# Mixing y as it is loaded, and sharing the mixing of x among three engines: a batched product x·yᵀ on one core

## The chip, the core and the metric

The kernel runs on one core of a Trainium2 chip. The metric is the device time in microseconds of one execution. The kernel before takes 303.1 us (three runs, 302.90 to 303.12). The span of a profile, counted from the first to the last recorded instruction, is slightly shorter (300.9 us for the kernel before).

## The reference

```python
batch, n_heads, seq_t, seq_s, channels = 8, 12, 512, 512, 64
# x, y: (8, 12, 512, 64) float32
def reference(x, y):
    return np.einsum('bhtc,bhsc->bhts', x, y).astype(np.float32)
```

There are 96 products of 512 x 64 by 64 x 512. The inputs have 25.2 MB, the output has 100.7 MB. The arithmetic is small: what counts is moving 125.8 MB. In the kernel before TensorE is busy with matmuls for 46% of the span, and the DMA queue fills 98.5% of it.

## The kernel before

Eight heads are one group; there are 12 groups, each made of two half groups (24 in all, numbered i), and each half group gives two results of 2 MB (48 in all). x and y of a group are loaded into one **slot**. There are five slots, and results are written into slots too, from which they are stored. The kernel's matmuls take the channels on the partitions, so x and y are rearranged ("mixed") within a partition by strided copies and then transposed on VectorE (2.06 us for one xT, 1.05 for one yT).

```python
    slots = ctx.enter_context(tc.tile_pool(name="slots", bufs=SLOTS))      # SLOTS = 5
    zeroed = [const.tile([P, K * E * D], u32, name=f"xb{half}") for half in range(2)]

    def load(g):
        both = slot()
        nc.sync.dma_start(both[:, :R * C], xv[g])
        nc.sync.dma_start(both[:, R * C:], yv[g])
        loaded[g] = both

    def compress(g):                       # frees the slot: ScalarE reads x, VectorE reads y
        both = loaded.pop(g)
        xk = kept.tile([P, R, C], bf16)
        yk = kept.tile([P, R, C], bf16)
        nc.scalar.activation(xk.rearrange("p r c -> p (r c)"), both[:, :R * C], COPY)
        nc.vector.tensor_copy(yk.rearrange("p r c -> p (r c)"), both[:, R * C:])
        inputs[g] = (xk, yk)

    def mix(i):                            # GpSimd alone: 4 copies of x, 2 of y
        # ... 4 x nc.gpsimd.tensor_copy(xb part <- xk part, 32 x 1024)
        # ... 2 x nc.gpsimd.tensor_copy(yb part <- yk part, 64 x 1024)

    def transposes(i):                     # VectorE: xT <- xb, yT <- yb
        # ...
        if i + 2 < 2 * NG:
            mix(i + 2)

    def result(o):                         # 8 matmuls, 4 evictions into a slot, then a store
        i, h = divmod(o, 2)
        otf = slot()
        # ... evictions of k = 0, 2, 6 on ScalarE, of k = 4 on VectorE
        if h == 0 and 2 <= i + 2 < 2 * NG:
            transposes(i + 2)
        return lambda: nc.sync.dma_start(ov[i, h], otf)

    with tc.manual_schedule():             # each engine's order is the order written here
        for g in range(SLOTS):
            load(g)
        # ... zeroing of xb
        stores = []
        for g in range(NG):
            compress(g)
            if g == 0:
                mix(0)
                mix(1)
            if g in (2, 4):
                transposes(g // 2 - 1)
            if g < 5:
                load(g + SLOTS)
            elif g in (5, 7, 9):
                stores.append(result(len(stores)))
            elif g in (6, 8):
                load(g // 2 + 7)           # groups 10 and 11
        for store in stores:
            store()
        for o in range(len(stores), 4 * NG):
            result(o)()
```

In the traces every engine runs its list in the order written (GpSimd in the kernel before: x copies from 7.51 us, y copies from 13.85, the next x copies from 17.47). And all loads and stores go through one queue (q1 of the page, 125.83 MB), in which the first stores stand behind the last load, that of group 11 (y issued at 50.41, the first store at 50.88).

Of the kernel before, what the change touches and what calls it, by code (L numbers as in the profile page):

```python
# [1 line left out]

# [4 lines left out]


@with_exitstack
def kernel(  # L10
    ctx: ExitStack,
    tc: tile.TileContext,
    x: bass.AP,
    y: bass.AP,
    out: bass.AP,
):









    nc = tc.nc
    B, H, T, C = x.shape
    _, _, S, _ = y.shape
    P = 128
    G = 8  # L30
    Q = P // G
    R = T // Q
    NG = B * H // G
    K = 8
    E = R // K
    D = 32
    SLOTS = 5
    fp32 = mybir.dt.float32
    bf16 = mybir.dt.bfloat16
    u32 = mybir.dt.uint32  # L40
    COPY = mybir.ActivationFunctionType.Copy
    assert C == 2 * D and S == T and R == D and Q * 2 == D

    xv = x.rearrange("b h t c -> (b h t c)").rearrange("(g p n) -> g p n", p=P, n=R * C)
    yv = y.rearrange("b h t c -> (b h t c)").rearrange("(g p n) -> g p n", p=P, n=R * C)
    ov = out.rearrange("b h t s -> (b h t s)").rearrange(
        "(o u h q n) -> o h q u n", u=2, h=2, q=Q * E, n=K * S
    )

    const = ctx.enter_context(tc.tile_pool(name="const", bufs=1))  # L50
    kept = ctx.enter_context(tc.tile_pool(name="kept", bufs=NG))
    slots = ctx.enter_context(tc.tile_pool(name="slots", bufs=SLOTS))
    ybpool = ctx.enter_context(tc.tile_pool(name="ybpool", bufs=2))
    tpool = ctx.enter_context(tc.tile_pool(name="tpool", bufs=3))
    pmpool = ctx.enter_context(tc.tile_pool(name="pmpsum", bufs=4, space=bass.MemoryType.PSUM))

    loaded, inputs, mixed, made = {}, {}, {}, {}
    zeroed = [const.tile([P, K * E * D], u32, name=f"xb{half}") for half in range(2)]

    def slot():  # L60
        return slots.tile([P, K * S], fp32, name="slot")
# [5 lines that stand above are left out]
        loaded[g] = both  # L67

    def compress(g):
        both = loaded.pop(g)  # L70
        xk = kept.tile([P, R, C], bf16)
        yk = kept.tile([P, R, C], bf16)
        nc.scalar.activation(xk.rearrange("p r c -> p (r c)"), both[:, :R * C], COPY)  # L73
        nc.vector.tensor_copy(yk.rearrange("p r c -> p (r c)"), both[:, R * C:])  # L74
        inputs[g] = (xk, yk)

    def mix(i):

        g, half = divmod(i, 2)
        xk, yk = inputs[g]  # L80
        xb = zeroed[half]
        xv2 = xb.bitcast(bf16).rearrange("p (k e c u) -> p k e c u", k=K, e=E, u=2)
        base = half * 64
        for ch in range(2):
            for u in range(2):
                lo = base + u * D
                nc.gpsimd.tensor_copy(  # L87
                    xv2[(2 * ch + u) * D:(2 * ch + u + 1) * D, :, :, :, u],
                    xk[lo:lo + D, :, ch * D:(ch + 1) * D].rearrange("p (e k) c -> p k e c", k=K),
                )  # L90
        yb = ybpool.tile([P, R // 2 * D], u32)
        yv2 = yb.bitcast(bf16).rearrange("p (j c w) -> p j w c", j=R // 2, w=2)
        for ch in range(2):
            nc.gpsimd.tensor_copy(  # L94
                yv2[ch * 64:(ch + 1) * 64],
                yk[base:base + 64, :, ch * D:(ch + 1) * D].rearrange("p (j w) c -> p j w c", w=2),
            )
        mixed[i] = (xb, yb)

    def transposes(i):  # L100
        xb, yb = mixed.pop(i)
        xT = tpool.tile([P, K * D * E], u32)
        nc.vector.transpose(  # L103
            xT.rearrange("p (k r e) -> p k e r", k=K, e=E),
            xb.rearrange("p (k e c) -> p k e c", k=K, e=E),
        )
        yT = tpool.tile([P, D * R // 2], u32)
        nc.vector.transpose(  # L108
            yT.rearrange("p (r j) -> p j r", r=D), yb.rearrange("p (j c) -> p j c", c=D)
        )  # L110
        made[i] = (xT.bitcast(bf16).rearrange("p (k h m) -> p k h m", k=K, h=2), yT.bitcast(bf16))
        if i + 2 < 2 * NG:
            mix(i + 2)

    def result(o):

        i, h = divmod(o, 2)
        xT, yT = made[i]
        otf = slot()
        ot = otf.rearrange("p (r s) -> p r s", s=S)  # L120
        for k in range(0, K, 2):
            pm = pmpool.tile([P, 2, S], fp32)
            for two in range(2):
                nc.tensor.matmul(  # L124
                    pm[:, two, :], xT[:, k + two, h, :], yT[:, h * S:(h + 1) * S], start=True, stop=True
                )
            if k == 4:
                nc.vector.tensor_copy(ot[:, k:k + 2, :], pm)  # L128
            else:
                nc.scalar.activation(ot[:, k:k + 2, :], pm, COPY)  # L130
        if h == 0 and 2 <= i + 2 < 2 * NG:
            transposes(i + 2)
        return lambda: nc.sync.dma_start(ov[i, h], otf)

    with tc.manual_schedule():
        for g in range(SLOTS):
            load(g)
        nc.vector.memset(zeroed[0], 0.0)  # L138
        nc.gpsimd.memset(zeroed[1], 0.0)  # L139
# [5 lines that stand above are left out]
                mix(1)  # L145
            if g in (2, 4):
                transposes(g // 2 - 1)
            if g < 5:
                load(g + SLOTS)
            elif g in (5, 7, 9):  # L150
                stores.append(result(len(stores)))
            elif g in (6, 8):
                load(g // 2 + 7)
# [6 lines that stand above are left out]
# [1 line left out]
_INS = ['x', 'y']  # L161
_OUTS = [((8, 12, 512, 512), 'float32')]


# [23 lines left out]
```

## Time and profile before

| | kernel before |
|---|---|
| time | 303.1 us |
| span of the profile | 300.9 us |
| the DMA queue's share of 16 engines' span | 98.5% |
| GpSimd busy | 202.4 us (67%) |
| ScalarE busy | 160.7 us (53%) |
| VectorE busy | 148.0 us (49%) |

A page of the profile cuts the span into 40 slices. A digit is the busy share of a slice in tenths, and the row GB/s is what the DMA moved in it. A row of a group reads: line, engine, operation, output <- input, shapes, count, then busy microseconds and mean nanoseconds of one, then the idle time in front of it and what ended it. A row of the timeline begins with start and duration in us. The lines themselves are in the prediction.

### The profile page before, as it was taken

How to read it: one execution, taken by the hardware profiler on the slowest of the kernel's cores; microseconds unless marked ns; L12 is line 12 of the kernel's file. 1: busy time of each engine (PE TensorE's matmuls, PEld its weight loads, DVE VectorE, ACT ScalarE, POOL GpSimd, SP SyncE). 2: the span in 40 equal slices, each digit the busy share in tenths (PEclk: the TensorE clock that was granted, in tenths of full speed). 3: DMA queues.
4: the chain of work that ended last, by engine and by line, in shares of the span. 5: the costliest groups of instructions: out<-in, count | busy, mean ns of one | idle time of the engine just before them, and what ended most of it. 6: DMA issues, size and time to landing. Idle time of an engine off the chain costs nothing.

```text
span 300.9 us, 1567 instructions
## 1 busy us (share of the span) xinstructions
PE 137.7 (46%) x377; PEld 46.9 (16%) x384; DVE 148.0 (49%) x109; ACT 160.7 (53%) x157; POOL 202.4 (67%) x149
## 2 busy tenths in 40 slices
PE   0004124465465456664646664547555845654000
PEld 0001001122121112221212121212121212211000
DVE  1565963858375546653574356535753475313000
ACT  4252558697473747465655565655556564647000
POOL 1999999998997787779776977797779720000000
PEclk9999987579877885577895586797785598775555
DMA  7999999999999999999999999999999999999993
GB/s 293 424 426 424 421 419 423 424 441 423 441 425 423 438 425 431 436 425 440 425 429 439 420 431 433 427 442 423 429 437 423 433 433 423 430 429 425 431 429 150
DMA packets 10377, 125.93 MB, mean 418 GB/s; under 512 B 1152, under 2 KB 1152, under 8 KB 1152
## 3 DMA queue, kind: packets, MB, share of 16 engines
q1 hardware_dynamic: 10368, 125.83, 98.5%
q8 instruction: 3, 0.05, 0.1%
q14 instruction: 6, 0.05, 0.0%
HBM read 25.17 MB, written 100.66 MB: 418 GB/s over the span
## 4 chain that ended last, share of the span: by engine, by line
DMA 82%; ACT 7%; issue 3%; ACTq 0%; DVE 0%; SPq 0%
DMA out_dram<-slot 65%; DMA slot<-in_y_dram 17%; ACT slot L130 7%; DVE yk L74 0%; ACTq L183 0%; SPq L65 0%; SPq L66 0%; ACTq L130 0%
## 5 line engine op out<-in xcount | busy, mean ns | idle before, releaser
L124 PE MATMUL pm<-yT,xT 128*128 128x512 bf16 x377 | 137.7, 516 | 137.9 <-ACT slot L130 112.5
L130 ACT ACTIVATE slot<-pm 128x1024 f32<-128x1024 f32 x144 | 137.0, 1024 | 96.2 <-DMA out_dram<-slot 88.3
L87 POOL COPY xb<-xk 32x1024 bf16<-32x1024 bf16 x96 | 134.5, 1401 | 37.1 <-DVE xT L103 27.5
L128 DVE COPY slot<-pm 128x1024 f32<-128x1024 f32 x48 | 58.7, 1224 | 101.5 <-DMA out_dram<-slot 100.4
L124 PEld LDWEIGHTS <-xT 128*128 128x128 bf16 x384 | 46.9, 122 | 227.7 <-issue 193.0
L94 POOL COPY yb<-yk 64x1024 bf16<-64x1024 bf16 x48 | 66.8, 1391 | 2.9
L103 DVE STREAM_TRANSPOSE xT<-xb 128x1024 uint32<-128x1024 uint32 x24 | 49.5, 2063 | 0.0
L73 ACT ACTIVATE xk<-slot 128x2048 bf16<-128x2048 f32 x12 | 23.0, 1913 | 21.1 <-DMA slot<-in_x_dram 21.1
L74 DVE CAST yk<-slot 128x2048 bf16<-128x2048 f32 x12 | 20.6, 1715 | 26.6 <-DMA slot<-in_y_dram 26.6
L108 DVE STREAM_TRANSPOSE yT<-yb 128x512 uint32<-128x512 uint32 x24 | 25.3, 1052 | 0.0
L73 ACT ACT_TABLE_LOAD x1 | 1.3, 1283 | 0.7 <-PEq L172 0.7
L138 DVE MEMSET xb<- 128x1024 uint32 x1 | 0.9, 912 | 1.0 <-PEq L172 1.0
L139 POOL MEMSET xb<- 128x1024 uint32 x1 | 1.0, 952 | 0.3 <-POOLq L172 0.3
L172 POOL MEMSET const-float32-0.0<- 128x1 f32 x1 | 0.1, 98 | 0.2 <-issue 0.2
L172 POOL MEMSET const-float32-1.0<- 128x1 f32 x1 | 0.1, 98 | 0.0
L172 POOL MEMSET const-bfloat16-1.0<- 128x1 bf16 x1 | 0.1, 98 | 0.0
L172 POOL MEMSET const-uint8-127<- 128x1 uint8 x1 | 0.1, 98 | 0.0
## 6 DMA issues: line engine op xcount, KB each, us to landing
out_dram<-slot SPq DMA_DIRECT2D x48, 2048.0 KB, 21.7
slot<-in_x_dram SPq DMA_DIRECT2D x12, 1024.0 KB, 18.1
slot<-in_y_dram SPq DMA_DIRECT2D x12, 1024.0 KB, 19.2
```

The source lines that it names most:

```text
L73: nc.scalar.activation(xk.rearrange("p r c -> p (r c)"), both[:, :R * C], COPY)
L74: nc.vector.tensor_copy(yk.rearrange("p r c -> p (r c)"), both[:, R * C:])
L87: nc.gpsimd.tensor_copy(xv2[(2 * ch + u) * D:(2 * ch + u + 1) * D, :, :, :, u], xk[lo:lo + D, :, ch * D:(ch + 1) * D].rearrange("p (e k) c ...
L94: nc.gpsimd.tensor_copy(yv2[ch * 64:(ch + 1) * 64], yk[base:base + 64, :, ch * D:(ch + 1) * D].rearrange("p (j w) c -> p j w c", w=2),)
L103: nc.vector.transpose(xT.rearrange("p (k r e) -> p k e r", k=K, e=E), xb.rearrange("p (k e c) -> p k e c", k=K, e=E),)
L108: nc.vector.transpose(yT.rearrange("p (r j) -> p j r", r=D), yb.rearrange("p (j c) -> p j c", c=D))
L124: nc.tensor.matmul(pm[:, two, :], xT[:, k + two, h, :], yT[:, h * S:(h + 1) * S], start=True, stop=True)
L128: nc.vector.tensor_copy(ot[:, k:k + 2, :], pm)
L130: nc.scalar.activation(ot[:, k:k + 2, :], pm, COPY)
L138: nc.vector.memset(zeroed[0], 0.0)
L139: nc.gpsimd.memset(zeroed[1], 0.0)
L172: nc = _bacc.Bacc("TRN2", target_bir_lowering=False, num_devices=1)
```

## The change

The intent is to relieve GpSimd, the busiest engine, which did all the mixing. The halves of y are now mixed straight out of the fp32 slot while loading: per group VectorE makes two copies, GpSimd one and ScalarE one. x of the first five half groups is still mixed by GpSimd. From the sixth on, VectorE makes two of the four copies, GpSimd one and ScalarE one. The mixing of x also moves within the order: from the transposes to the load stage and to behind each second result. `copy` in the cut below is a helper that calls `activation` on ScalarE and `tensor_copy` on the other engines; " ..." marks what is left out.

```diff
+    in_front = [nc.vector, nc.gpsimd, nc.vector, nc.scalar]
+    behind = [nc.vector, nc.gpsimd, nc.scalar, nc.vector]
 ...
     def compress(g):
         both = loaded.pop(g)
         xk = kept.tile([P, R, C], bf16)
-        yk = kept.tile([P, R, C], bf16)
         nc.scalar.activation(xk..., both[:, :R * C], COPY)
-        nc.vector.tensor_copy(yk..., both[:, R * C:])
+        ys = both[:, R * C:].rearrange("p (r c) -> p r c", c=C)
+        for half in range(2):
+            yb = kept.tile([P, R // 2 * D], u32, name=f"yb{half}")
+            for ch in range(2):
+                copy(in_front[2 * half + ch], yb part, ys part)
 ...
     def mix(i):
         for ch in range(2):
             for u in range(2):
-                nc.gpsimd.tensor_copy(xb part, xk part)
+                copy(nc.gpsimd if i < 5 else behind[2 * ch + u], xb part, xk part)
-        # two nc.gpsimd.tensor_copy of y
 ...
     def transposes(i):
-        if i + 2 < 2 * NG:
-            mix(i + 2)
 ...
     def result(o):
-        if h == 0 and 2 <= i + 2 < 2 * NG:
+        if h == 0 and i + 2 < 2 * NG:
             transposes(i + 2)
+        elif h == 1 and i + 4 < 2 * NG:
+            mix(i + 4)
 ...
             if g in (2, 4):
                 transposes(g // 2 - 1)
+                mix(g // 2 + 1)
```

More of the change, by code (lines that the diff above doesn't have):

```diff
@@ L52 @@
     slots = ctx.enter_context(tc.tile_pool(name="slots", bufs=SLOTS))
-    ybpool = ctx.enter_context(tc.tile_pool(name="ybpool", bufs=2))
     tpool = ctx.enter_context(tc.tile_pool(name="tpool", bufs=3))
@@ L58, with copy @@
     zeroed = [const.tile([P, K * E * D], u32, name=f"xb{half}") for half in range(2)]
+    in_front = [nc.vector, nc.gpsimd, nc.vector, nc.scalar]
+    behind = [nc.vector, nc.gpsimd, nc.scalar, nc.vector]
+    def copy(engine, dst, src):
+        if engine is nc.scalar:
+            nc.scalar.activation(dst, src, COPY)
+        else:
+            engine.tensor_copy(dst, src)
     def slot():
@@ L71, in compress @@
         xk = kept.tile([P, R, C], bf16)
-        yk = kept.tile([P, R, C], bf16)
         nc.scalar.activation(xk.rearrange("p r c -> p (r c)"), both[:, :R * C], COPY)
-        nc.vector.tensor_copy(yk.rearrange("p r c -> p (r c)"), both[:, R * C:])
-        inputs[g] = (xk, yk)
+        inputs[g] = xk
+        ys = both[:, R * C:].rearrange("p (r c) -> p r c", c=C)
+        for half in range(2):
+            yb = kept.tile([P, R // 2 * D], u32, name=f"yb{half}")
+            yv2 = yb.bitcast(bf16).rearrange("p (j c w) -> p j w c", j=R // 2, w=2)
+            for ch in range(2):
+                copy(
+                    in_front[2 * half + ch],
+                    yv2[ch * 64:(ch + 1) * 64],
+                    ys[half * 64:(half + 1) * 64, :, ch * D:(ch + 1) * D].rearrange(
+                        "p (j w) c -> p j w c", w=2
+                    ),
+                )
+            mixed[2 * g + half] = yb
     def mix(i):
         g, half = divmod(i, 2)
-        xk, yk = inputs[g]
-        xb = zeroed[half]
-        xv2 = xb.bitcast(bf16).rearrange("p (k e c u) -> p k e c u", k=K, e=E, u=2)
-        base = half * 64
+        xk = inputs[g]
+        xv2 = zeroed[half].bitcast(bf16).rearrange("p (k e c u) -> p k e c u", k=K, e=E, u=2)
         for ch in range(2):
             for u in range(2):
-                lo = base + u * D
-                nc.gpsimd.tensor_copy(
+                lo = half * 64 + u * D
+                copy(
+                    nc.gpsimd if i < 5 else behind[2 * ch + u],
                     xv2[(2 * ch + u) * D:(2 * ch + u + 1) * D, :, :, :, u],
@@ L90, in mix @@
                 )
-        yb = ybpool.tile([P, R // 2 * D], u32)
-        yv2 = yb.bitcast(bf16).rearrange("p (j c w) -> p j w c", j=R // 2, w=2)
-        for ch in range(2):
-            nc.gpsimd.tensor_copy(
-                yv2[ch * 64:(ch + 1) * 64],
-                yk[base:base + 64, :, ch * D:(ch + 1) * D].rearrange("p (j w) c -> p j w c", w=2),
-            )
-        mixed[i] = (xb, yb)
     def transposes(i):
-        xb, yb = mixed.pop(i)
+        xb, yb = zeroed[i % 2], mixed.pop(i)
         xT = tpool.tile([P, K * D * E], u32)
```

## The prediction

The sum came to 307.0 us: 303.1 for the kernel before, and 3.85 us of starvation. "Lock" is the word for the time that a copy of one engine adds to a copy of the other; the traces show that time and not the mechanism behind it. That the new VectorE copies (the "them" behind the second cut) add it as the CAST does was an assumption, and 0.4 us for each was estimated from the 0.9 of the CAST. Rival A is the case that they add nothing.

> **What bounds the kernel now.** I read the page first (slices, queues, chain of waits), then the groups by line, the waits of the DMA queue, and the timeline of the first 64 us, where the change acts most.
>
> From the page:
>
> ```profile
> DMA  7999999999999999999999999999999999999993
> GB/s 293 424 426 424 421 419 423 424 441 423 441 425 423 438 425 431 436 425 440 425 429 439 420 431 433 427 442 423 429 437 423 433 433 423 430 429 425 431 429 150
> ...
> q1 hardware_dynamic: 10368, 125.83, 98.5%
> ...
> DMA 82%; ACT 7%; issue 3%; ACTq 0%; DVE 0%; SPq 0%
> ...
> L87 POOL COPY xb<-xk 32x1024 bf16<-32x1024 bf16 x96 | 134.5, 1401 | 37.1 <-DVE xT L103 27.5
> ...
> L94 POOL COPY yb<-yk 64x1024 bf16<-64x1024 bf16 x48 | 66.8, 1391 | 2.9
> ...
> out_dram<-slot SPq DMA_DIRECT2D x48, 2048.0 KB, 21.7
> ```
>
> The DMA rows carry the verdict: between first and last slice no slice falls under 9 tenths, and the one busy queue fills 98.5% of 16 engines' span. 125.83 MB at the 420 to 442 GB/s of the middle slices is some 290 to 295 us of a 300.9 us span; the rest is start and tail. GpSimd, busiest of the engines (202.4 us, 67%), is not the bound. A store lands 21.7 us after its issue although 2 MB at 430 GB/s takes 4.9 us, so about four transfers are always queued: in the store stage an engine may be many microseconds late and the DMA notices nothing. Relieving GpSimd therefore buys nothing by itself. The change can only move the time by letting the DMA queue run empty, and that must be looked for in the load stage, where queue and slots are shared by loads and first results.
>
> The timeline, first its issues and landings, then single GpSimd and VectorE instructions:
>
> ```profile
> 0.74 0.39 SPq L65 DMA_DIRECT2D slot<-in_x_dram  x1
> 5.54 1.91 ACT L73 ACTIVATE xk<-slot 128x2048 bf16<-128x2048 f32 x1 [3.53 <-DMA slot<-in_x_dram]
> 8.00 1.90 DVE L74 CAST yk<-slot 128x2048 bf16<-128x2048 f32 x1 [6.07 <-DMA slot<-in_y_dram]
> ...
> 32.86 2.05 DVE L74 CAST yk<-slot 128x2048 bf16<-128x2048 f32 x1 [0.18 <-DMA slot<-in_y_dram]
> 35.07 2.85 ACT L130 ACTIVATE slot<-pm 128x1024 f32<-128x1024 f32 x3 [2.77 <-DVE yk L74]
> ...
> 40.28 0.33 SPq L65 DMA_DIRECT2D slot<-in_x_dram  x1
> ...
> 50.04 0.33 SPq L65 DMA_DIRECT2D slot<-in_x_dram  x1
> ...
> 60.21 1.91 ACT L73 ACTIVATE xk<-slot 128x2048 bf16<-128x2048 f32 x1 [1.41 <-DMA slot<-in_x_dram]
> ```
>
> ```profile
> 7.51 1.31 POOL L87 COPY xb<-xk 32x1024 bf16<-32x1024 bf16 x1 [5.83 <-ACT xk L73]
> 8.86 2.22 POOL L87 COPY xb<-xk 32x1024 bf16<-32x1024 bf16 x1
> ...
> 47.77 1.23 DVE L74 CAST yk<-slot 128x2048 bf16<-128x2048 f32 x1 [1.16 <-DMA slot<-in_y_dram]
> ```
>
> Read there: a load issued alone at 0.74 lands at 5.54, 4.8 us. One y lands every 4.97 us (8.00 for group 0, 32.86 for group 5). Group 5's slot is free at 34.9 and goes to result 0 at 35.07. The last two loads are issued at 40.28 (group 10) and 50.04 (group 11), and x of group 11 lands at 60.21 in an unbroken stream. So it must be issued by about 60.2 - 4.8 = 55.4; before, there are 5.4 us to spare. The stores are issued only behind these loads, in program order, so nothing else can fill a hole.
>
> [...] a GpSimd copy takes 1.31 us, but 2.22 where a CAST became ready at 8.00; the CAST takes 1.90 there, 1.23 at 47.77. Each CAST costs GpSimd 0.9 us. [...] I take them to lock as the CAST does; no run yet shows it. [...]
>
> **The change part by part.**
> Removed: 12 VectorE casts (20.6 us) and 48 GpSimd y copies (66.8 us). Added: 48 y copies out of the fp32 slot, 24 on VectorE, 12 on ScalarE, 12 on GpSimd. The 96 x copies stay, but GpSimd does 4 x 5 + 19 = 39, VectorE 38, ScalarE 19. Estimates for one: VectorE 0.6 us (half of 1.23), [...] GpSimd 1.35 (from start to start, 7.51 to 8.86). GpSimd falls to about 51 x 1.35 = 69 us, [...] VectorE gains 62 x 0.6 - 20.6 = 17 us. All stay well under the span. Per pair of results, 9.8 us of DMA, VectorE needs 2 x 1.22 + 2.06 + 1.05 + 2 x 0.6 = 6.8 [...]. So the store stage is still hidden: worth nothing either way.
>
> Moved: a slot is now free only when GpSimd too has copied its y part out of it. GpSimd works in order, and its list puts the x copies of the first five half groups between: y0, mix 0, mix 1, y1, y2, mix 2, y3, y4, mix 3, y5, y6, y7, mix 4, y8. Up to y5 that is 16 + 6 = 22 copies, 22 x 1.36 = 29.9 us from 8.0. To it come the locks of 12 VectorE copies: the CAST cost 0.9, one of half the length about 0.4, in sum 4.8. So y5 ends at about 8.0 + 29.9 + 4.8 = 42.7, and result 0, which needs this slot, starts there in place of 35.07.
>
> Behind it ScalarE and VectorE also work in order. ScalarE: result 0 42.8 to 45.7, x6 to 47.6, [...]. VectorE: eviction to 44.0, transposes (2.05 + 1.05) to 47.2, then four y copies of groups 6 and 7, alternating with the copies of mix 4 on GpSimd, which starts when the first transpose frees xb at 46.2: they end at about 48.1, 49.8, 51.6 and 53.3. Group 6's slot is free at 49.8, so load 10 is issued then: 49.8 + 4.8 = 54.6, while unbroken its x would land at 60.2 - 4.97 = 55.2. Just in time. Result 1 needs group 7's slot: ScalarE 53.4 to 56.25, x8 to 58.15, [...]. Only now is group 8's slot free for load 11: issued at 59.25, x landed at 64.05 against 60.2. **The DMA is starved for 3.85 us** around 57 to 61 us. After that results 0 and 1 are ready to go, and each further result needs 2.85 us of evictions against 4.9 of transfer, so the queue fills again and the loss is neither repeated nor won back.
>
> Sum: 303.1 + 3.9 = 307.0 us.
>
> **The rivals.**
> A: no loss. [...] y5 ends at 37.9, load 11 is issued 4.8 us earlier still through ScalarE's chain [...], inside 55.4, and the time is 303. For it: the destination has a step of 4 bytes, unlike the CAST. [...]
> B: a larger loss. If the two engines alternate worse (0.55 per lock) or GpSimd's fp32 source costs it more than 1.35, y5 ends at 44 to 45, load 10 is late by 1 as well and load 11 by 5: 308.5 to 310.
> C: a gain, since GpSimd is 67% busy and loses 130 us of work. Against it: the DMA rows; the most that is left is start and tail, which the change does not touch. 302 to 303.
> D: the store stage starves as VectorE gets the x copies. Against it: 6.8 of 9.8 us and four queued stores.
>
> **Range and chances.** The step in the middle has a width of about 2 us: without the wait for group 7's copies on VectorE the hole is 2 us, with worse alternation 5.5. Rival A gets 15 to 20%, so the range reaches down to it: 302.8 to 309.3. 2% slower is 309.2, the upper end of rival B: 0.13. 2% faster would be 297, which leaves the DMA a span of 295 us, its bare 290 to 295 without start and tail: 0.01. Within 2%: 0.86.
>
> **What would show it.** In the changed profile: result 0's first eviction at about 43 and not at 35; the loads of groups 10 and 11 issued at about 50 and 59; in the slices a dip of DMA and GB/s in the eighth or ninth (52 to 68 us), some 4 us deep, and none later; in the queue's waits ScalarE or GpSimd of the y copies as what the last load waited for; GpSimd copies at 1.7 us in the load stage, 1.31 later; VectorE y copies of 0.6 us alone and up to 1.9 contended; store latency again about 21.7. I am wrong if the DMA rows have no dip (rival A or C), if load 11 is issued before 55, or if a dip lies in the store stage (D).

## The result

The changed kernel takes 308.24 us (median of four runs, 307.99 to 308.51), beside 303.01 us for the kernel before on the same chip. The ratio is 1.0174, with a 95% interval from 1.0156 to 1.0192. Ratios in this document are the mean time of one kernel's fast runs over the mean of the other's of the same rounds, so they are not quite the ratio of the medians quoted. The loss of 1.7% is under 2%, but it is far outside the noise.

From the page of the changed kernel, the slices, the queue and the groups that answer to those shown of before:

```profile
DMA  7999999499999999999999999999999999999994
GB/s 288 427 422 424 421 421 409 200 325 430 425 439 421 434 434 421 443 419 436 435 419 443 421 432 434 424 443 417 437 425 432 434 424 430 428 426 439 417 436 205
...
q1 hardware_dynamic: 10368, 125.83, 97.3%
...
L66 POOL COPY xb<-xk 32x1024 bf16<-32x1024 bf16 x39 | 57.0, 1461 | 147.5 <-DVE xT L114 146.5
...
L66 DVE CAST yb<-slot 64x1024 bf16<-64x1024 f32 x24 | 33.2, 1384 | 12.6 <-DMA slot<-in_y_dram 12.3
...
L66 DVE COPY xb<-xk 32x1024 bf16<-32x1024 bf16 x38 | 27.8, 732 | 0.5
...
L66 POOL CAST yb<-slot 64x1024 bf16<-64x1024 f32 x12 | 17.7, 1511 | 17.7 <-DMA slot<-in_y_dram 17.5
L64 ACT ACTIVATE yb<-slot 64x1024 bf16<-64x1024 f32 x12 | 15.9, 1326 | 3.6 <-DMA slot<-in_y_dram 3.4
...
out_dram<-slot SPq DMA_DIRECT2D x48, 2048.0 KB, 21.6
```

The DMA row has one dip, in the eighth slice (a slice is 7.66 us, so 53.6 to 61.3 us); the GB/s stay low through the ninth. Before and behind it the rows read as in the kernel before, and a store still lands 21.6 us after its issue. GpSimd is indeed relieved, from 202.4 us busy to 75.9, and the time went up.

The timeline of the changed kernel, its results, loads and the copies between:

```profile
43.39 2.85 ACT L139 ACTIVATE slot<-pm 128x1024 f32<-128x1024 f32 x3 [9.09 <-POOL yb L66]
...
50.65 0.33 SPq L73 DMA_DIRECT2D slot<-in_x_dram  x1
...
54.16 2.85 ACT L139 ACTIVATE slot<-pm 128x1024 f32<-128x1024 f32 x3 [1.35 <-DVE yb L66]
...
58.97 1.33 ACT L64 ACTIVATE yb<-slot 64x1024 bf16<-64x1024 f32 x1
...
60.37 0.33 SPq L73 DMA_DIRECT2D slot<-in_x_dram  x1
```

Read these as a chain. ScalarE sits idle for 9.09 us before result 0, until GpSimd's y copy of group 5 has read the slot; the result starts at 43.39 where it started at 35.07 before. Result 1 follows at 54.16, held by VectorE's y copies of group 7. ScalarE's y copy of group 8 ends at 60.30, and only then is the load of group 11 issued, at 60.37 where it was 50.04.

The waits of the changed kernel's DMA queue (waited for: us in total, times, longest) name the same holders:

```profile
SPq L73 <- DVE yb L66: 24.2, 4, 13.6
...
SPq L73 <- POOL yb L66: 17.7, 4, 8.8
...
SPq L73 <- ACT yb L64: 2.5, 1, 2.5
```

Nine waits of the loads now end with some engine's y copy; the one load that waited for ScalarE is the last. Most of this waiting is harmless, since the DMA was busy all the same: the DMA row has a 9 in every slice but the first, the eighth and the last.

What it costs is seen by stretches. The columns are the stretch, its length, each engine's busy time and instructions, the granted TensorE clock, the DMA's busy share and its GB/s. The kernel before:

```profile
57.00:62.00 5.00, 1.79 (x5) 0.47 (x4) 2.29 (x3) 3.59 (x2) 4.86 (x4) 0.76 1.03 431
62.00:70.00 8.00, 5.62 (x17) 1.95 (x18) 6.69 (x6) 8.00 (x10) 6.71 (x5) 0.79 1.03 442
80.00:280.00 200.00, 113.52 (x309) 38.48 (x313) 100.28 (x76) 114.64 (x121) 132.10 (x101) 0.74 1.01 430
```

The changed kernel:

```profile
57.00:62.00 5.00, 1.55 (x5) 0.43 (x4) 3.29 (x4) 4.93 (x4) 1.79 (x1) 0.84 0.16 33
62.00:70.00 8.00, 3.57 (x8) 1.13 (x8) 6.25 (x6) 7.82 (x8) 0.83 (x1) 0.60 1.01 363
80.00:280.00 200.00, 112.41 (x330) 39.00 (x337) 133.35 (x118) 143.85 (x145) 23.81 (x18) 0.80 1.01 430
```

In the 5 us from 57 to 62 the DMA moves 33 GB/s in place of 431, which is 5 x 398 / 430 = 4.6 us of transfer lost. In the 8 us behind, it is busy but moves 363 in place of 442, another 8 x 79 / 430 = 1.5 us. Together that is 6.1 us; the span grew by 5.5 us, and the 0.6 us between them are not accounted for. In the 200 us of the store stage both move 430 GB/s, although VectorE and ScalarE carry 30 us more each there.

### The profile page after: what moved, and what is told of

Same layout as the page of the kernel before. It is cut to its first block, busy times and chain, and to the rows that moved or that the text cites. A ratio compares the mean times of both kernels' runs of the same rounds, so it can differ in the third digit from the quotient of the medians.

```text
span 306.4 us, 1486 instructions
## 1 busy us (share of the span) xinstructions
PE 132.8 (43%) x377; PEld 45.5 (15%) x384; DVE 188.9 (62%) x159; ACT 202.2 (66%) x188; POOL 75.9 (25%) x56
## 4 chain that ended last, share of the span: by engine, by line
DMA 56%; ACT 15%; issue 1%; ACTq 0%
DMA out_dram<-slot 56%; ACT slot L139 12%; ACT xk L81 1%; ACT yb L64 1%; ACT xb L64 1%; ACTq L195 0%; ACTq L139 0%
## 5 line engine op out<-in xcount | busy, mean ns | idle before, releaser
L133 PE MATMUL pm<-yT,xT 128*128 128x512 bf16 x377 | 132.8, 496 | 148.2 <-ACT slot L139 115.9
L66 POOL COPY xb<-xk 32x1024 bf16<-32x1024 bf16 x39 | 57.0, 1461 | 147.5 <-DVE xT L114 146.5
L133 PEld LDWEIGHTS <-xT 128*128 128x128 bf16 x384 | 45.5, 119 | 234.6 <-issue 196.9
L114 DVE STREAM_TRANSPOSE xT<-xb 128x1024 uint32<-128x1024 uint32 x24 | 49.8, 2076 | 0.7
L66 DVE CAST yb<-slot 64x1024 bf16<-64x1024 f32 x24 | 33.2, 1384 | 12.6 <-DMA slot<-in_y_dram 12.3
L66 DVE COPY xb<-xk 32x1024 bf16<-32x1024 bf16 x38 | 27.8, 732 | 0.5
L64 ACT ACTIVATE xb<-xk 32x1024 bf16<-32x1024 bf16 x19 | 25.4, 1335 | 0.5
L66 POOL CAST yb<-slot 64x1024 bf16<-64x1024 f32 x12 | 17.7, 1511 | 17.7 <-DMA slot<-in_y_dram 17.5
L64 ACT ACTIVATE yb<-slot 64x1024 bf16<-64x1024 f32 x12 | 15.9, 1326 | 3.6 <-DMA slot<-in_y_dram 3.4
## 6 DMA issues: line engine op xcount, KB each, us to landing
out_dram<-slot SPq DMA_DIRECT2D x48, 2048.0 KB, 21.6
```

Source lines behind the costliest of these rows:

```text
L64: nc.scalar.activation(dst, src, COPY)
L66: engine.tensor_copy(dst, src)
L114: nc.vector.transpose(xT.rearrange("p (k r e) -> p k e r", k=K, e=E), xb.rearrange("p (k e c) -> p k e c", k=K, e=E),)
L133: nc.tensor.matmul(pm[:, two, :], xT[:, k + two, h, :], yT[:, h * S:(h + 1) * S], start=True, stop=True)
```

## The experiments

**The theory:** the time is that of the DMA, and the change costs one hole in its queue, because the last load is issued too late. It is late because a slot now waits for GpSimd's in-order list, and behind it for ScalarE's and VectorE's. **Rival 1:** the store stage pays, as VectorE and ScalarE carry the x copies there. **Rival 2:** the engines' accesses slow the transfers themselves. A further question was how much of GpSimd's delay comes from its list and how much from copies that take longer beside VectorE's (2.22 us in place of 1.31 in the kernel before).

| run | what | time | before, same rounds | ratio [95%] | last load issued |
|---|---|---|---|---|---|
| – | the changed kernel | 308.24 | 303.01 | 1.0174 [1.0156, 1.0192] | 60.37 |
| e1 | store 0 ahead of the last load | 303.64 | 303.07 | 1.0027 [1.0006, 1.0048] | 60.30 |
| e2 | y part alone | 308.39 | 303.07 | 1.0183 [1.0166, 1.0200] | 60.42 |
| e3 | x part alone | 302.76 | 303.07 | 0.9990 [0.9975, 1.0005] | 50.09 |
| e4 | GpSimd mixes 3 half groups of x, not 5 | 306.10 | 303.07 | 1.0100 [1.0085, 1.0115] | 57.46 |
| e5 | no y copies on VectorE | 314.86 | 303.26 | 1.0385 [1.0369, 1.0400] | 64.74 |
| e6 | no y copies on GpSimd | 304.18 | 303.26 | 1.0040 [1.0024, 1.0055] | 55.98 |
| e7 | kernel before, store 0 ahead | 303.37 | 303.26 | 1.0007 [0.9990, 1.0023] | 50.40 |
| e8 | kernel before, slot of group 8 held longer | 307.79 | 303.26 | 1.0152 [1.0136, 1.0167] | 58.76 |
| e9 | e1 and e6 together | 303.03 | 302.88 | 0.9998 [0.9981, 1.0014] | 55.91 |

All gave correct results. e1 to e4 ran on one chip, e5 to e8 on another, e9 on a third; each is compared with the kernel before on its own chip.

### e1: one DMA issue moved

```diff
             elif g in (6, 8):
+                if g == 8:
+                    stores.pop(0)()
                 load(g // 2 + 7)
 ...
```

(Cut: the numbers of the results, which the kernel takes from the length of `stores`, are written out in two more lines.)

> The changed kernel with one DMA issue moved: the store of result 0 goes out ahead of the last load (group 11). All engine instructions stay as they are. My theory (one hole in the DMA queue, because the last load is issued at 60.4 while the loads before it end at 58.0): result 0 is evicted at 46.3 in the profile of the changed kernel, so its store (4.9 us of DMA) can be issued right behind load 10 at about 51.5 and bridges 58.0 to 62.9; the last load still goes out at about 60.4. The dip in the slices is gone and the time is 302.8 to 303.6, within 0.2% of before. Rival 1 (the store stage pays, as VectorE and ScalarE carry more there): nothing changes, 308. Rival 2 (the transfers themselves are slowed by more engine accesses): nothing changes, 308.

The time is 303.64 us, the engines' instructions being those of the changed kernel in the same order. The timeline of the queue:

```profile
51.41 0.64 SPq L144 DMA_DIRECT2D out_dram<-slot  x1
60.30 0.33 SPq L73 DMA_DIRECT2D slot<-in_x_dram  x1
```

The last load is as late as before the edit, and nearly all of the loss is gone. So the engines' work and their collisions cost time only through the hole: what counts is whether the DMA has something to do from 57 to 62 us. Rivals 1 and 2 fall. The time is just above the range that I had expected, and 0.6 us above the kernel before; e7 and e9 take that up. Also missed: the dip in the slices is not gone. The DMA is busy throughout, but the eighth slice moves 317 GB/s:

```profile
GB/s 295 432 419 428 422 416 419 317 416 436 426 432 429 434 429 434 425 436 427 426 436 432 434 421 432 432 429 425 435 420 432 434 419 434 429 425 427 423 438 217
```

### e2 and e3: one part of the change at a time

```diff
 # e2
-                    nc.gpsimd if i < 5 else behind[2 * ch + u],
+                    nc.gpsimd if i < 24 else behind[2 * ch + u],
```

> The y part of the change alone: y is mixed at load by three engines as in the changed kernel, but GpSimd does all 24 half groups of x, so VectorE and ScalarE do no x copies. My theory: until 60 us the instruction lists are those of the changed kernel, so the same hole: 308.0 to 308.6, last load issued at 60.4. Rival 1 (the store stage pays for the x copies on VectorE and ScalarE): these are gone, 303 to 305.

e3 takes y back to the way of the kernel before (one cast per group on VectorE while loading, the two strided copies on GpSimd later) and leaves the sharing of x as changed.

```diff
 # e3, in compress and mix (shortened)
-        # four copies of y out of the slot, on three engines
+        yk = kept.tile([P, R, C], bf16)
+        nc.vector.tensor_copy(yk..., both[:, R * C:])
 ...
+            nc.gpsimd.tensor_copy(yb part, yk part)     # twice per half group
```

> The x part alone: x copies shared as in the changed kernel, y as before (VectorE casts the whole group at load, GpSimd mixes it later out of the bf16 copy). My theory: a slot is free again as soon as ScalarE and VectorE have read it, result 0 starts at about 35, the last load goes out at about 50, no hole: 302.8 to 303.6. Rival 1 (store stage): 307 to 308.

e2 gives 308.39 us, the whole loss, though all x copies are back on GpSimd. e3 gives 302.76 us, with x shared through the whole store stage: the same as before within the noise. The loss is in the y part, and nothing of it is in the store stage.

### e4: a dose

```diff
-                    nc.gpsimd if i < 5 else behind[2 * ch + u],
+                    nc.gpsimd if i < 3 else behind[2 * ch + u],
```

> A dose: GpSimd alone mixes x of 3 half groups in place of 5; the others are shared 2:1:1. My theory: 3 copies fewer on GpSimd before y of group 5 (3 x 1.36 = 4.1 us, less the locks of two more VectorE copies): it ends at about 39.5 in place of 43.4. Behind it one more copy of 1.33 on ScalarE and fewer locks: last load at about 56.4 in place of 60.4, the hole is about 1 us in place of 5: 303.6 to 305. Rivals 1 and 2: more copies on VectorE and ScalarE, so 308 or more.

The direction is right, the size was missed: 306.10 us, where I expected 303.6 to 305. From the timeline of e4:

```profile
38.53 1.74 DVE L66 CAST yb<-slot 64x1024 bf16<-64x1024 f32 x1
...
40.56 1.23 DVE L137 COPY slot<-pm 128x1024 f32<-128x1024 f32 x1 [0.30 <-DVE yb L66]
```

GpSimd's list is shorter, but the two x copies that VectorE got stand ahead of its y copies of group 5. Each of these four runs beside GpSimd's copies and takes 1.6 to 1.75 us, so the slot comes free at 40.3 by VectorE, after GpSimd's copy, which ended at 39.7 (I had worked out 39.5). The last load went out at 57.46 where I had worked out 56.4. I had counted the delay for GpSimd and not for VectorE.

### e5: how much VectorE's copies slow GpSimd's

```diff
-    in_front = [nc.vector, nc.gpsimd, nc.vector, nc.scalar]
+    in_front = [nc.scalar, nc.gpsimd, nc.scalar, nc.scalar]
```

> The changed kernel with the two y copies of VectorE per group given to ScalarE, so that VectorE runs no SBUF copy in the load stage. [...] My theory: every GpSimd copy up to y of group 5 takes 1.31 (in the changed kernel about half took 1.7 to 1.8), so it ends at 8.2 + 22 x 1.36 = 38.1 in place of 43.4. The time gets worse all the same, since ScalarE now needs 1.91 + 3 x 1.33 = 5.9 us per group against 4.97 of loading: y of group 5 ends there at 41.6, and through its list (result 0, x6, y6, x7, y7, result 1, x8, y8) the last load is issued at 65.0, some 9.8 us after the 55.2 at which it would still be seamless: 312.5 to 314. Rival (GpSimd's order alone decides, no lock): GpSimd's copies keep their 1.7 to 1.8.

GpSimd's first two copies in the timeline of the changed kernel (the second row merges two):

```profile
8.22 1.78 POOL L66 CAST yb<-slot 64x1024 bf16<-64x1024 f32 x1 [6.54 <-DMA slot<-in_y_dram]
10.06 3.06 POOL L66 COPY xb<-xk 32x1024 bf16<-32x1024 bf16 x2
```

The same in e5, and the copies of y of groups 5 and 6 (merged in the last row):

```profile
8.14 1.30 POOL L66 CAST yb<-slot 64x1024 bf16<-64x1024 f32 x1 [6.46 <-DMA slot<-in_y_dram]
9.50 2.66 POOL L66 COPY xb<-xk 32x1024 bf16<-32x1024 bf16 x2
...
36.53 2.67 POOL L66 CAST yb<-slot 64x1024 bf16<-64x1024 f32 x2
```

Without a VectorE copy beside it, each GpSimd copy takes 1.31 us, and y of group 5 ends at about 37.9. In the changed kernel it ends at about 43.4. The difference of 5.5 us is what VectorE's copies cost GpSimd; the prediction estimated 4.8 for it. So of the 8.3 us by which result 0 starts later than in the kernel before (43.39 beside 35.07), about 5.5 come from the two engines slowing each other and only 2.8 from the length of GpSimd's list. The time, 314.86 us, is worse than the 312.5 to 314 expected. The last load went out at 64.74, as worked out (65.0). But in e5's page the twelfth slice is low as well:

```profile
GB/s 291 432 420 420 423 424 421 117 206 379 436 320 434 417 418 436 429 415 431 433 431 419 426 429 431 419 425 432 431 415 433 431 430 417 423 431 433 421 429 283
```

A second hole near 86 to 94 us (320 in place of about 430 in a slice of 7.8 us, so 2 us) is large enough for what I had missed. The timeline of e5 shows what came before it: ScalarE was still copying y until 85.1, evicted result 3 only from 85.12 on, and its store went out at 88.01, 14 us behind the store of result 2. My sum stopped at the last load.

### e6: GpSimd out of the slot's way

```diff
-    in_front = [nc.vector, nc.gpsimd, nc.vector, nc.scalar]
+    in_front = [nc.vector, nc.scalar, nc.vector, nc.scalar]
```

> The changed kernel with GpSimd's y copy given to ScalarE (VectorE and ScalarE two each), so that a slot no longer waits for GpSimd. If GpSimd's in-order list were the whole cause: result 0 starts at 36.7 and the time is 303. By my arithmetic ScalarE's list then becomes the limit: result 0 36.7 to 39.6, x6 41.5, two y6 44.2, x7 46.1, two y7 48.7, result 1 51.6, x8 53.5, two y8 56.1: last load at about 56.2, 1 us late, plus up to 1 us for loads and stores that start together: 304 to 305.

The time is 304.18 us, inside the range worked out. From the timeline of e6:

```profile
36.38 2.86 ACT L139 ACTIVATE slot<-pm 128x1024 f32<-128x1024 f32 x3 [0.74 <-DVE yb L66]
...
49.75 1.50 DVE L66 CAST yb<-slot 64x1024 bf16<-64x1024 f32 x2
...
53.29 2.67 ACT L64 ACTIVATE yb<-slot 64x1024 bf16<-64x1024 f32 x2
55.98 0.33 SPq L73 DMA_DIRECT2D slot<-in_x_dram  x1
```

Result 0 starts at 36.4, 7 us sooner, and still the last load is late by half a microsecond: ScalarE's own list is now what holds the slot of group 8. So waiting for GpSimd's copy is the larger cause, but not the only one. In each of the three ways of sharing the four y copies that were run (the changed kernel, e5, e6) a slot comes free too late for the last load, as it did not with the one cast on VectorE. The row at 49.75 shows two y copies of VectorE with GpSimd idle: 0.75 us each.

### e7 and e8: the kernel before, with one thing done to it

e7 makes the same edit as e1 in the kernel before.

> The kernel before with the store of result 0 ahead of the last load, as in e1. There was a residue of 0.6 to 1 us in e1, and in e1, e4 and the changed kernel the GB/s fall to 180 to 370 for some 4 us when loads and stores are issued within a microsecond of each other onto a nearly empty queue. Here the queue is deep: the store is issued at about 41, 16 us ahead of its turn. If mixing loads and stores itself costs, 303.6 to 304.5; if only the late issue costs (my guess), 302.8 to 303.3.

The time is 303.37 beside 303.26 us, a hair above my guess and inside the noise: a store among the loads cost nothing that shows here, where it was issued at 41.22, 9.2 us ahead of the last load (50.40), and the DMA was busy throughout.

e8 lengthens the hold on the slot of group 8, by repeating a copy with the same result.

```diff
-        nc.scalar.activation(xk.rearrange("p r c -> p (r c)"), both[:, :R * C], COPY)
+        for _ in range(6 if g == 8 else 1):
+            nc.scalar.activation(xk.rearrange("p r c -> p (r c)"), both[:, :R * C], COPY)
```

> The kernel before with nothing of the change: ScalarE makes its bf16 copy of x of group 8 six times in place of once (same result), so that the slot comes free 9.6 us later and the last load is issued at about 59.6 in place of 50.0. No GpSimd or VectorE work changes. My theory (the late issue of the last load is sufficient): a hole of 59.6 - 55.2 = 4.4 us and up to 1 us more, 307 to 308.5, with the same dip in the slices. If the change cost through anything else, this stays near 303.

The time is 307.79 us. ScalarE in the timeline of e8 (five repeats merged with the copies of groups 8 and 9), and the load behind it:

```profile
47.10 13.43 ACT L74 ACTIVATE xk<-slot 128x2048 bf16<-128x2048 f32 x7
58.76 0.33 SPq L65 DMA_DIRECT2D slot<-in_x_dram  x1
```

The stretches of e8, with the columns as above:

```profile
57.00:62.00 5.00, 0.36 (x1) 0.10 (x1) 1.44 (x2) 4.97 (x4) 1.16 (x1) 0.50 0.42 143
62.00:70.00 8.00, 5.13 (x12) 1.57 (x11) 6.76 (x5) 7.77 (x8) 6.07 (x4) 0.50 1.01 371
```

None of the change is in this kernel: GpSimd mixes everything, y is cast by VectorE. A late last load alone makes the same hole (5 x 288 / 430 = 3.3 us) and a like slow spell behind it (8 x 71 / 430 = 1.3 us), and 4.5 us of time. The repeats also push ScalarE's later work back (result 2 starts at 60.56 beside 54.14), but from 70 to 80 us the DMA moves 431 GB/s, so nothing shows that this costs more. So the late load is sufficient, as e1 showed that filling the hole is enough to undo the loss.

### e9: both repairs

The edit is that of e1 and that of e6.

> The changed kernel with both repairs: GpSimd's y copy goes to ScalarE (as in e6) and the store of result 0 goes out ahead of the last load (as in e1). In e6 load 10 was issued at 43.9 and result 0 evicted at 39.3, so the store follows at about 44.7, 13 us ahead of its turn, as in e7; the last load is issued at about 56 with the store still to run until 63. No hole, no late issue onto an empty queue: 302.8 to 303.4, equal to the kernel before. If the store stage of the changed kernel cost anything, it would be what is left over here: over 303.5.

The time is 303.03 beside 302.88 us, a ratio of 0.9998. Thus the sharing of x, with y shared between VectorE and ScalarE, costs nothing that shows once the queue stays fed, and it gains nothing either. For y with GpSimd's part in it the nearest run is e1, with 0.6 us left. No version here beats the kernel before by more than the noise; e3 has the lowest median, and its interval includes 1.

## Why the prediction was right

The time was predicted as 307.0 us, in a range from 302.8 to 309.3, and came out as 308.24.

**The bound.** The reading that relieving GpSimd could gain nothing held: 126.5 us less work on it, and the rate in the store stage is 430 GB/s in both kernels. Single slices reach 442 (the kernel before) and 443 (the changed kernel).

**GpSimd's list up to y of group 5.** Predicted end 42.7, measured about 43.4. The lock term was 4.8 and measured as 5.5 (e5). The open point of rival A, whether the new VectorE copies slow GpSimd's at all, is settled: a y copy takes 0.75 us with GpSimd idle (e6; 0.6 was predicted) and 1.74 beside it (e4), and a GpSimd copy goes from 1.31 (e5) to 1.78 (the changed kernel, at 8.22). So rival A was wrong. Rival B was in part right: the alternation was somewhat worse than in the main line.

**The chain to the last load.** Predicted: result 0 at 42.8, load 10 at 49.8, result 1 at 53.4, last load at 59.25. Measured: 43.39, 50.65, 54.16, 60.37. Of the last 1.1 us, 0.75 are inherited from GpSimd's end and VectorE's slowed copies. The rest arose behind result 1, where ScalarE's y copy of group 8 took 1.33 us; the prediction's term for it came from no run and was too short. The dense copy of 2048 elements takes ScalarE 1.91 us, the y and x copies of 1024 elements 1.33 and 1.34.

**The hole.** The sum had 3.85 us of starvation; the time grew by 5.2. The 1.1 us of lateness above bring the sum to 4.95, which leaves 0.3. What the sum had no term for is a slow spell: the loads and the first stores are issued within a few microseconds, the DMA is busy, and yet it moves 363 GB/s over 8 us, which the stretches count as 1.5 us. Most of that lies from 65 to 68 us, with 273 GB/s at a busy share of 1.02, beside 426 in the kernel before. As hole and spell together come to more than the span grew, how much of the spell reaches the time is open.

The spell appears some 4.5 to 5.5 us after the issue of the late load in every one of these kernels whose stretches were read: 273 GB/s from 65 to 68 us in the changed kernel (last load issued at 60.37), 219 from 62 to 65 in e4 (57.46), 213 from 70 to 72 in e5 (64.74), 262 from 61 to 64 in e6 (55.98), 217 from 64 to 66 in e8 (58.76). The DMA's busy share is 0.81 there in e5 and 0.91 to 1.02 in the others. It appears in e1 too, with hardly a gap before it: after load 10 and the store right behind it, issued at 50.56 and 51.41, the DMA moves 311 GB/s from 54 to 60 us at a busy share of 0.99. It is absent in e7, where the store was issued early: between the first and the last slice the GB/s stay at 420 to 441. What makes it was not tested; the 0.6 us left in e1 may be its cost. If the latest seamless issue is taken as 55.4, as the prediction has it, the lateness and the loss in median time are 5.0 and 5.2 us for the changed kernel, 2.1 and 3.0 for e4, 3.4 and 4.5 for e8, 0.6 and 0.9 for e6; e5 with its second hole has 9.3 and 11.6. (The 4.8 us in that 55.4 are not quite those of a load issued alone: seven more were issued by 4.40.)

**The store stage** was predicted to be worth nothing, and e2, e3 and e9 show it, although the copies were under-counted: VectorE gained 40.9 us of work where 17 were predicted, and ScalarE 41.5. A y copy of VectorE took 1.38 us on average and an x copy 0.73, not 0.6. There was room for it, as the prediction said of this stage.

## What to carry to other kernels

In a kernel bound by transfers, do not ask which engine is busiest, but how early each transfer is issued and which instruction it waits for. Here a buffer that three engines read came free only when the last of them had come to it in its own in-order list, which held much work that has nothing to do with the buffer: ScalarE sat idle for 9.09 us before result 0. Where transfers are issued in the order of the program, the DMA can be kept fed by putting one that is ready ahead of one that will be late; here one moved line took 308.24 us to 303.64, nearly all of a loss that the engines' busy times do not show.
